# Tile columns of a two-layer encoder rounded up so that operands of full products start on 256-byte multiples

## The chip, the core and the metric

The kernel runs on one core of one Trainium2 chip. The metric is device time in microseconds (us) of one launch. Five engines work side by side: TensorE (PE in the profile; its weight loads stand under PEld), VectorE (DVE), ScalarE (ACT), GpSimd (POOL) and SyncE (SP, which only issues transfers here). TensorE reads both operands of a product from SBUF, the on-chip memory of 128 partitions, and writes to PSUM. A tile takes the same byte range in every partition, so its place is one number, its start within a partition. "Residue" below means this start modulo 256 bytes.

## The reference

Two layers of a transformer encoder over 256 tokens of width 1024, everything in float32. Each layer has a mixer and a channel part:

```
h    = rms_norm(x, n1); proj = h @ w_in                 # 1024 -> 2560
a: 4 heads, neighbourhood window with a bias table; q,k normed per head
d: 6 heads, three dilated windows joined by their log-sum-exp; partial rotary
c: 6 query heads on 2 key heads, full softmax; axial rotary
mix  = concat(rms_norm(out_a), rms_norm(out_d), rms_norm(out_c)) * gains
x    = x + mix @ w_out                                  # 1024 -> 1024
h    = rms_norm(x, n2); g, u = split(h @ w_gate_up)     # 1024 -> 2 x 2816
g    = depthwise_conv(g, 3 taps along the tokens) + conv_b
x    = x + (gelu(g) * u) @ w_down                       # 2816 -> 1024
```

## The kernel before, in words

Every large product is made in three terms. An operand z is split into z_hi, its value rounded to the type float32r, and z_lo = z - z_hi, also float32r; the product is hi·hi + hi·lo + lo·hi, added up in PSUM. The weights stream in from HBM in units of up to 2048 columns (tiles `wp_raw0` to `wp_raw3`); ACT rounds each unit into `wp_hi` and DVE subtracts into `wp_lo` (two buffers each, function `split`, lines 717 to 736). The profile names a product as output<-moving operand,stationary operand. These are the products of TensorE:

- Projections (lines 943 to 959): moving `wp_hi`/`wp_lo` with 384, 256 or 512 columns, stationary a 128x128 piece of `act_hT`, output in `psa_a`.
- Attention: transposes against `const_ident`, scores over 64 partitions (`act_ko`, `act_qo`, `act_kc`, `act_qc`), and weighted values (`act_pT` moving, `const_v` stationary), which are plain float32 and stand in the profile as two records each.
- Output projection (lines 967 to 984): moving `wp_hi`/`wp_lo` with 512 columns (in layer 2 partly `act_kc`/`act_qc`, reused as weight tiles), stationary `act_mixT_hi`/`act_mixT_lo`.
- Feed-forward up (lines 1370 to 1405, gate and up halves): a "large" term, moving `act_hT` with 512 columns (hi and lo side by side), stationary `wp_hi`, followed per output by a "little" term, moving 256 columns of `act_hT`, stationary `wp_lo`; eight of each per output half, in `psw_w`.
- Feed-forward down (lines 1457 to 1477): moving `wp_hi`/`wp_lo` with 512 columns, stationary `act_ch`/`act_cl`, the split activation; output in `psa_a`, one accumulation over all steps. The last piece is cut into 256 columns (line 1463).

The class `Plan` records all operations first, orders them with a cost model and a hand-tuned table of offsets (`PLACES`), and then emits them engine by engine (`order` and `emit`). It knows nothing of addresses. A tile's real place is taken at first use in `Slots.place` (lines 180 to 186), one allocation per buffer, sized in columns by the widest tile of that tag:

```
shape = list(t.shape) if self.dram else [P, BANK if self.psum else self.cols]
```

Allocations of SBUF follow one another, pool by pool (`const`, `wp`, `act`, `small`), each rounded up to 32 bytes. In the built program the first tile, `warm`, starts at byte 16512, and a few tiles whose size is no multiple of 256 bytes (`mh` 128 bytes, `gains` 192, `rot` 1664, `fo` one element, `few` 124, `sdq` and `sdk` 128, `cw` 352) shift everything behind them. Adding up the sizes gives these residues before:

| tiles | part in products | residue before |
|---|---|---|
| `const_ident`, `const_x` | moving and stationary of transposes | 0 |
| `wp_hi`, `wp_lo`, `wp_raw` | stationary (up), moving (projections, output, down) | 96 |
| `act_hT` | moving (up), stationary (projections) | 96 |
| `act_qo`, `act_ko`, `act_qc`, `act_kc`, `act_pT` | scores, values, some of the output projection | 224 |
| `act_mixT_hi`, `act_mixT_lo` | stationary (output projection) | 224 |
| `const_v6`, `const_v2` | stationary of the weighted values | 64 |
| `act_ch`, `act_cl` | stationary (down) | 64 |

Slices inside these tiles that a product reads step by multiples of 256 bytes, so all pieces of a tile share its residue.

Of the kernel before, what the change touches and what calls it, by code (L numbers as in the profile page):

```python
# [18 lines left out]
P = 128  # L19
# [17 lines left out]
UNIT = 2048  # L37
BANK = 512
NS2K = 5
NPT = 9  # L40

TURN_ACT = ("d", "dca")
# [128 lines left out]
class Slots:  # L171
# [7 lines left out]

    def place(self, t):  # L180
        if t.slot not in self.places:
            shape = list(t.shape) if self.dram else [P, BANK if self.psum else self.cols]
            self.places[t.slot] = self.pool.real.tile(
                shape, self.dtype, tag=f"{self.tag}{t.slot}", name=f"{self.pool.name}_{self.tag}{t.slot}", bufs=1
            )
        return self.places[t.slot]
# [86 lines left out]
class Plan:  # L273
# [5 lines left out]
    def pool(self, real, name, bufs, space=bass.MemoryType.SB):  # L279
        return PlanPool(self, real, name, bufs, space)  # L280
# [76 lines left out]
    def order(self):  # L357
# [82 lines left out]
        while len(done) < len(ops):  # L440
# [27 lines left out]
            for t in o.tiles:  # L468
                if t.slot is None:
                    s = t.pool  # L470
                    s.given += 1
                    place = min(s.free)
                    s.free.remove(place)
                    t.since, t.slot = taken_at(place[0], ""), place[1]
# [87 lines left out]
def encoder_kernel(  # L562
# [25 lines left out]
    const = pool("const", 1)  # L588
    wp = pool("wp", 3)
    act = pool("act", 2)  # L590
    small = pool("small", 4)
# [12 lines left out]

    gl0 = act.tile([16, P], F32, tag="s2k", name="gl0", bufs=NS2K)
    gl1 = act.tile([32, P], F32, tag="s2k", name="gl1", bufs=NS2K)
    gains = const.tile([P, 3, DEPTH, KD], F32, tag="gains", name="gains")
# [10 lines left out]
        nc.vector.tensor_copy(gains[:, i : i + n].rearrange("p a l k -> p (a l k)"), ps[:, :w])  # L618


    warm = const.tile([P, P], mybir.dt.bfloat16, tag="warm", name="warm")
    nc.gpsimd.memset(warm, 1.0)
    wps = psa.tile([P, WARM_W], F32, tag="a", name="wps")

# [163 lines left out]
    def mean_squares(name):  # L788

        ss = small.tile([P, NT, 2], F32, tag="ssx", name=f"ssx_{name}", bufs=2)  # L790
        for h in range(2):
            for t in range(NT):
                junk = act.tile([P, 512], F32, tag="s2k", name=f"sq_{name}{t}{h}", bufs=NS2K)
                nc.scalar.activation(
# [136 lines left out]
    for l in range(DEPTH):  # L931
# [84 lines left out]
        def normed(ps, nh, t, name):  # L1016

            w = nh * HD
            sq = act.tile([P, 512], F32, tag="s2k", name=f"sq_{name}", bufs=NS2K)
            ss = small.tile([P, 8], F32, tag="ss", name=f"ss_{name}")  # L1020
# [80 lines left out]
        class Head:  # L1101
# [4 lines left out]
            def softens(self, sps, whole):  # L1106

                name, bias = self.name, self.bias
                self.p = p = act.tile([P, NT, S], F32, tag="s2k", name=f"p_{name}", bufs=NS2K)
                nm = small.tile([P, NT], F32, tag="nm", name=f"nm_{name}")  # L1110
                rs = small.tile([P, NT], F32, tag="rs", name=f"rs_{name}")

                if bias is not None:
                    sb = act.tile([P, NT, S], F32, tag="s2k", name=f"sb_{name}", bufs=NS2K)
                    for t in range(NT):
# [22 lines left out]
            def turn(self):  # L1138
# [7 lines left out]
                odd = self.h % 2  # L1146
                self.pT = act.tile([P, NT, S], F32, tag="pT", name=f"pT_{name}", bufs=NPT)
                with nc.later(TURN_LATER):
# [436 lines left out]
```

## Time and profile before

| | us |
|---|---|
| median of 3 runs (lowest, highest) | 605.46 (604.07, 605.92) |
| the profiled execution, own time | 605.0 |
| its span, first to last instruction | 603.0 |
| PE busy in the span | 595.2 |
| PEld, DVE, ACT, POOL busy | 511.5, 471.1, 413.3, 78.0 |

The program runs on one core, and the granted TensorE clock is 1.000 over the whole span. A product's duration in the profile covers its pass through the array, and successive products overlap in it; the pace of a stream is read from the starts of its first and of the next product, divided by their count. The chain of waits merges neighbouring products to such pieces (start, length, count).

### The profile page before, as it was taken

The numbers are of one execution on the slowest core, as the hardware profiler recorded it, in microseconds if no ns is written. First come the engines' busy times: TensorE is split into PE (matmuls) and PEld (weight loads), VectorE is DVE, ScalarE is ACT, GpSimd is POOL, SyncE is SP. The second block draws the span as 40 slices with busy tenths as digits, with TensorE's granted clock in tenths as the row PEclk, the third lists the DMA queues.
The fourth block names the chain that finished last, engine by engine and source line by source line (L and its number), as shares of the span: only waits on it lengthen the run. The fifth ranks groups of instructions, "written<-read, shape, count | busy, mean of one in ns | idle before, by whom it ended". The sixth has DMA issues, their size and how long they took to land.

```text
span 603.0 us, 9676 instructions
## 1 busy us (share of the span) xinstructions
PE 595.2 (99%) x3423; PEld 511.5 (85%) x3423; DVE 471.1 (78%) x983; ACT 413.3 (69%) x1035; POOL 78.0 (13%) x124
## 2 busy tenths in 40 slices
PE   7999999999999999999999999999999999999997
PEld 6998787788888888888899988778888888888886
DVE  2788989897779797987977897668976677767875
ACT  4798989586575685756777898676765555646651
POOL 0652140160000000000014213421000000000000
PEclk9999999999999999999999999999999999999999
DMA  8896323555679898988635826944465455745511
GB/s 276 264 230 193 106 88 109 193 186 181 225 222 281 255 365 298 345 312 275 218 107 173 277 74 245 304 154 139 147 203 174 165 161 199 254 164 193 162 65 71
DMA packets 85216, 121.43 MB, mean 201 GB/s; under 512 B 9880, under 2 KB 69880, under 8 KB 85168
## 3 DMA queue, kind: packets, MB, share of 16 engines
q1 hardware_dynamic: 82992, 112.22, 57.2%
q0 software_dynamic: 1728, 8.39, 4.0%
q8 instruction: 27, 0.44, 0.3%
q10 hardware_dynamic: 448, 0.20, 0.1%
q14 instruction: 21, 0.17, 0.1%
HBM read 110.93 MB, written 9.88 MB: 200 GB/s over the span
## 4 chain that ended last, share of the span: by engine, by line
PE 92%; DMA 3%; DVE 2%; ACT 1%; issue 0%; POOL 0%; ACTq 0%; SPq 0%; DVEq 0%
PE psw_w L514 50%; PE psa_a L514 42%; DMA act_nab<-dram_scr 2%; DMA const_x<-in_x_dram 1%; DMA dram_scr<-act_nab 1%; DVE wp_lo L514 1%; ACT act_s2k L514 0%; DVE act_z L514 0%; DVE act_nab L514 0%; POOL small_rstd L514 0%; ACT wp_hi L514 0%; DVE act_sw L514 0%; ACT act_hT L514 0%; ACTq L514 0%; DVE act_s2k L514 0%
## 5 line engine op out<-in xcount | busy, mean ns | idle before, releaser
L514 DVE TENSOR_TENSOR wp_lo<-wp_raw,wp_hi 128x512 fp32r<-128x512 f32 (+2 forms) x332 | 233.8, 736 | 34.8 <-ACT wp_hi L514 19.3
L514 ACT CAST wp_hi<-wp_raw 128x512 fp32r<-128x512 f32 (+2 forms) x332 | 202.3, 666 | 19.0 <-PE psw_w L514 10.8
L514 PE MATMUL psw_w<-act_hT,wp_hi 128*128 128x512 f32 x704 | 182.8, 393 | 0.0
L514 PEld LDWEIGHTS psw_w<-act_hT,wp_hi 128*128 128x128 f32 x704 | 128.3, 188 | 23.9
L514 PE MATMUL psa_a<-wp_hi,act_hT 128*128 128x384 f32 (+2 forms) x448 | 114.6, 336 | 0.6 <-ACT wp_hi L514 0.6
L514 PEld LDWEIGHTS psw_w<-act_hT,wp_lo 128*128 128x128 f32 x704 | 100.2, 190 | 8.2
L514 PE MATMUL psw_w<-act_hT,wp_lo 128*128 128x256 f32 x704 | 105.2, 282 | 0.0
L514 PEld LDWEIGHTS psa_a<-wp_hi,act_hT 128*128 128x128 f32 x448 | 79.4, 191 | 3.8 <-ACT wp_hi L514 0.7
L514 PE MATMUL psa_a<-wp_lo,act_hT 128*128 128x384 f32 (+2 forms) x224 | 75.3, 338 | 0.0
L514 ACT COPY act_s2k<-psw_w 128x256 f32<-128x256 f32 x88 | 31.7, 372 | 57.5 <-PE psw_w L514 57.1
L514 DVE TENSOR_TENSOR act_s2k<-psw_w,act_s2k 128x256 f32<-128x256 f32 x88 | 36.1, 421 | 42.4 <-ACT act_s2k L514 41.9
L514 PE MATMUL psa_a<-wp_lo,act_ch 128*128 128x512 f32 (+1 forms) x176 | 68.6, 392 | 0.0
L514 PE MATMUL psa_a<-wp_hi,act_cl 128*128 128x512 f32 (+1 forms) x176 | 67.9, 392 | 0.0
L514 PE MATMUL psa_a<-wp_hi,act_ch 128*128 128x512 f32 (+1 forms) x176 | 65.9, 393 | 0.0
L514 PEld LDWEIGHTS psa_a<-wp_lo,act_hT 128*128 128x128 f32 x224 | 42.8, 191 | 2.3 <-DVE wp_lo L514 1.0
L514 PEld LDWEIGHTS psa_a<-wp_hi,act_cl 128*128 128x128 f32 x176 | 33.0, 188 | 7.0
L514 PEld LDWEIGHTS psa_a<-wp_lo,act_ch 128*128 128x128 f32 x176 | 32.9, 188 | 6.6
L514 PEld LDWEIGHTS psa_a<-wp_hi,act_ch 128*128 128x128 f32 x176 | 32.9, 188 | 6.6
L514 DVE SCALAR_TENSOR_TENSOR act_s2k<-act_s2k,act_cw,act_s2k 128x255 f32<-128x255 f32 x88 | 37.1, 478 | 0.0
L514 ACT ACTIVATE act_s2k<-act_s2k 128x512 f32<-128x512 f32 x22 | 13.9, 632 | 31.4 <-DVE act_s2k L514 31.4
L514 ACT ACTIVATE act_s2k<-act_s2k,act_cw 128x256 f32<-128x256 f32 x44 | 24.1, 596 | 14.9 <-DVE act_s2k L514 14.8
L514 POOL TENSOR_TENSOR small_rstd<-small_ms,const_mh 128x6 f32<-128x6 f32 (+2 forms) x26 | 31.3, 1204 | 15.8 <-DVE small_ms L514 14.1
(129 smaller groups left out, 710.7 us busy)
## 6 DMA issues: line engine op xcount, KB each, us to landing
wp_raw<-in_w_gate_up_dram SPq DMA_DIRECT2D x44, 1024.0 KB, 5.2
wp_raw<-in_w_down_dram SPq DMA_DIRECT2D x22, 1024.0 KB, 5.4
wp_raw<-in_w_in_dram SPq DMA_DIRECT2D x14, 768.0 KB, 4.6
wp_raw<-in_w_in_dram SPq DMA_DIRECT2D x8, 1024.0 KB, 5.4
wp_raw<-in_w_out_dram SPq DMA_DIRECT2D x8, 768.0 KB, 6.5
dram_khi<-act_mixT_hi SPq DMA_DIRECT2D x4, 768.0 KB, 5.0
dram_klo<-act_mixT_lo SPq DMA_DIRECT2D x4, 768.0 KB, 8.3
wp_lo<-dram_klo POOLq DMA_DIRECT2D x4, 768.0 KB, 5.7
```

The source lines that it names most:

```text
L514: getattr(o.engine.real, o.method)(*map(real, o.args), **{k: real(v) for k, v in o.kw.items()})
```

## The change

The number of columns of each allocation in SBUF is rounded up to a multiple of 64 elements (256 bytes in four-byte types), for all pools but `small`. The tile `warm`, in two-byte elements, is allocated with 192 columns (384 bytes) of which 128 are used, so that what follows its start at 16512 begins at 16896.

```diff
@@ constants of the module
 NS2K = 5
+EVEN = 64
 NPT = 9
@@ Slots.place
         if t.slot not in self.places:
-            shape = list(t.shape) if self.dram else [P, BANK if self.psum else self.cols]
+            cols = self.cols if self.pool.name == "small" else -(-self.cols // EVEN) * EVEN
+            shape = list(t.shape) if self.dram else [P, BANK if self.psum else cols]
@@ encoder_kernel
-    warm = const.tile([P, P], mybir.dt.bfloat16, tag="warm", name="warm")
+    warm = const.tile([P, 3 * EVEN], mybir.dt.bfloat16, tag="warm", name="warm")[:, :P]
```

No instruction is added or taken away, and the order of the instructions on every engine is the same row for row. Shapes, strides and sizes of transfers are the same. The starts move up by 256 bytes (`const_ident`, `const_x`) to 1216 bytes (`act_ch`), and every tile of the pools `const` (but `warm`), `wp` and `act` then has residue 0. Distances between tiles change only where a rounded tile lies between them: `wp` and `act_hT` keep theirs (61440 bytes from `wp_hi0` to `act_hT`), while `act_mixT_hi` lies 384 bytes and `act_ch` 544 bytes farther from `wp_hi0`.

## The prediction

> **What bounds the kernel now.** I read the first lines of the page first, then what TensorE waited for, then its pace stage by stage from the chain of waits and the timeline.
>
> ```profile
> span 603.0 us, 9676 instructions
> PE 595.2 (99%) x3423; PEld 511.5 (85%) x3423; DVE 471.1 (78%) x983; ACT 413.3 (69%) x1035; POOL 78.0 (13%) x124
> PEclk9999999999999999999999999999999999999999
> ...
> PE psw_w L514 <- DMA const_x<-in_x_dram: 1.9, 1, 1.9
> PE psa_a L514 <- POOL const_mh L514: 1.0, 1, 1.0
> PE psa_a L514 <- ACT wp_hi L514: 0.6, 1, 0.6
> ...
> 200.00:250.00 50.00, 50.00 (x265) 42.80 (x264) 43.54 (x76) 34.48 (x64) 0.00 (x0) 1.00 0.89 305
> ```
>
> TensorE is busy for 595.2 of 603.0 us, and its longest waits are 1.9, 1.0 and 0.6 us, at the start. The clock is whole. The last row is a stretch in the feed-forward of layer 1 with the columns PE, PEld, DVE, ACT, POOL, clock, DMA share and GB/s: no hole in PE, while DVE has 6.5 us to spare in 50. So the kernel's time is the sum of the paces of TensorE's products, and a change of layout counts only through them. These groups hold most of the products:
>
> ```profile
> L514 PE MATMUL psw_w<-act_hT,wp_hi 128*128 128x512 f32 x704 | 182.8, 393 | 0.0
> L514 PE MATMUL psw_w<-act_hT,wp_lo 128*128 128x256 f32 x704 | 105.2, 282 | 0.0
> L514 PE MATMUL psa_a<-wp_hi,act_hT 128*128 128x384 f32 x256 | 68.4, 344 | 0.6 <-ACT wp_hi L514 0.6
> L514 PE MATMUL psa_a<-wp_lo,act_ch 128*128 128x512 f32 x172 | 67.4, 395 | 0.0
> L514 PE MATMUL psa_a<-wp_lo,act_mixT_hi 128*128 128x512 f32 x56 | 22.4, 401 | 0.0
> ```
>
> The large up terms are 704, the down terms 3 x 172 = 516 (the other two of the three have the same count), the output projection 3 x 56 = 168 and 24 more with reused tiles.
>
> Do these paces depend on residues? The kernel before is its own experiment, since moving and stationary operands have equal residues in some stages and unequal ones in others. Timeline rows give start, length and tiles of a product or a row of them; the two pieces of the chain give start, length and count.
>
> ```profile
> 160.18 2.88 PE L514 MATMUL psw_w<-act_hT,wp_hi 128*128 128x512 f32 x12
> 162.90 0.28 PE L514 MATMUL psw_w<-act_hT,wp_lo 128*128 128x256 f32 x1
> ...
> 208.72 2.00 PE L514 MATMUL psw_w<-act_hT,wp_hi 128*128 128x512 f32 x8
> 210.56 0.52 PE L514 MATMUL psw_w<-act_hT,wp_lo 128*128 128x256 f32 x3
> ...
> 295.11 9.33 PE psa_a L514 x40
> 310.37 14.33 PE psa_a L514 x81
> ...
> 404.29 0.40 PE L514 MATMUL psa_a<-wp_hi,act_mixT_hi 128*128 128x512 f32 x1
> 404.53 0.39 PE L514 MATMUL psa_a<-wp_lo,act_mixT_hi 128*128 128x512 f32 x1
> 404.76 0.40 PE L514 MATMUL psa_a<-wp_hi,act_mixT_lo 128*128 128x512 f32 x1
> 404.99 0.39 PE L514 MATMUL psa_a<-wp_hi,act_mixT_hi 128*128 128x512 f32 x1
> ...
> 409.05 0.62 PE L514 MATMUL psa_a<-act_kc,act_mixT_hi 128*128 128x512 f32 x2
> 409.50 0.39 PE L514 MATMUL psa_a<-act_kc,act_mixT_lo 128*128 128x512 f32 x1
> 409.73 0.62 PE L514 MATMUL psa_a<-act_kc,act_mixT_hi 128*128 128x512 f32 x2
> 410.18 0.39 PE L514 MATMUL psa_a<-act_kc,act_mixT_lo 128*128 128x512 f32 x1
> 410.41 0.39 PE L514 MATMUL psa_a<-act_qc,act_mixT_hi 128*128 128x512 f32 x1
> ```
>
> All of these but the 81 stream 512 columns. Up, residues 96 and 96: 12 products from 160.18 to 162.90, **226.7 ns each**. Down, residues 96 and 64: 40 products in 9.33 us, **233.3 ns**. Output projection with `wp`, residues 96 and 224: from 404.29 to 404.99 three products, 233 ns. The same stage with `act_kc` as the moving tile, residues 224 and 224: six products from 409.05 to 410.41, 226.7 ns. The last pair is the telling one: same stage, same stationary tile, same shape, only another moving residue. Equal residues go at 226.7 ns, unequal ones at 233. The rows from 208.72 show the limit: eight up products with equal residues take 1.84 us, 230.0 ns each. They follow little terms, and such a run begins slower before it settles: 8 x 3.3 = 27 ns lost per run.
>
> **The change part by part.** Nothing is added, removed or reordered, and no transfer has another size. What changes is where operands begin: every residue becomes 0.
>
> (a) Down, 516 products: residues 96/64 become 0/0, that is, equal. If the pace of equal residues holds at 0, each gains 233.3 - 226.7 = 6.6 ns, 3.4 us in all. Below that stands the loss at the beginning of runs: at worst each run loses 27 ns at its beginning, and in the timeline the down products stand in 48 runs, 1.3 us. Bounds: 2.1 to 3.4 us gained; I take 2.5, since many runs follow large terms, which leave the pace settled.
>
> (b) Output projection, 168 products: 96/224 become 0/0. At best 168 x 6.6 = 1.1 us, at worst nothing, because transposes break these runs up and each restart is unsettled. I take 0.4.
>
> (c) Up, projections and scores, with equal residues now and then: only the common residue moves, from 96 or 224 to 0. The trace has no float32r product at residue 0. Nearest are the equal pairs 96/96 and 224/224, which have one pace, so I take nothing. The bounds are the rivals B and D below.
>
> (d) Last piece of down, cut to 256 columns, 24 products. Unequal residues, 597.92 to 599.21, go a little faster than equal ones in the little terms:
>
> ```profile
> 530.54 1.96 PE L514 MATMUL psw_w<-act_hT,wp_lo 128*128 128x256 f32 x15
> 532.33 0.40 PE L514 MATMUL psw_w<-act_hT,wp_hi 128*128 128x512 f32 x1
> ...
> 597.92 0.28 PE L514 MATMUL psw_w<-wp_hi,act_ch 128*128 128x256 f32 x1
> 598.04 0.28 PE L514 MATMUL psw_w<-wp_lo,act_ch 128*128 128x256 f32 x1
> 598.15 0.28 PE L514 MATMUL psw_w<-wp_hi,act_cl 128*128 128x256 f32 x1
> 598.27 0.28 PE L514 MATMUL psw_w<-wp_hi,act_ch 128*128 128x256 f32 x1
> 598.39 0.28 PE L514 MATMUL psw_w<-wp_lo,act_ch 128*128 128x256 f32 x1
> ```
>
> 1.79 us for 15 is 119.3 ns; 0.47 us for four is 117. Made equal they lose 24 x 2.5 = 0.06 us.
>
> (e) Transfers, ACT and DVE also meet new residues. Cost nothing: the weight loads run ahead of a TensorE that never waits for them after its first microseconds, and DVE has 6.5 us in 50 as cover. With that cover gone, each us that DVE falls behind would be one of TensorE; I see no row that asks for it.
>
> Sum: -2.5 - 0.4 + 0.06 = -2.8 us against the profiled execution's 605.0 (603.0 span and 2.0 around it), so 602.2. The median of the runs shown lies 0.5 above this execution, so the forecast for the median is **602.6 us**. By (a) and (b) at their ends it is 601.0 to 603.4.
>
> **The rivals.** A is the sum above: equality of residues is what counts.
>
> B: the start itself counts, and residue 0 streams faster. For it: 226.7 ns for 512 columns is not the floor of this TensorE. The weighted values stream a plain float32 tile, in twelve products of two 256-column records:
>
> ```profile
> 77.13 2.81 PE L514 MATMUL psw_w<-act_pT,const_v 128*64 128x256 f32 x24
> ...
> 399.72 1.04 PE L514 MATMUL psw_w<-const_ident,act_s2k 128*128 128x128 f32 x8
> 400.52 0.48 PE L514 MATMUL psa_a<-wp_lo,act_mixT_hi 128*128 128x512 f32 x1
> ```
>
> Less about 0.39 for the last one's own passage this is 2.42 us for eleven intervals, 220 ns per 512 columns. Against it: `act_pT` lies at residue 224, so a bad start did not cost this stream anything, and the eight transposes (100 ns each, and all bound by their 128-column loads) have stationary residues of 96 and 224 without a visible price. If float32r products reached 220: up 704 x (228 - 220) = 5.6, down 516 x 13.3 = 6.9, the other 288 with 512 columns x 11 = 3.2, the 384 projections with 384 columns, from the 81 in 14.33 us (177 ns) to 220 x 3/4 = 165, 4.6, and the 896 with 256 columns from 119 towards 110 (220/2) at most 8. That is 20 to 28 us, 577 to 585, about **580**.
>
> [...]
>
> C: no residue counts, and the time stays at **605.4**. The paces above would then follow from the kind of product before and after, not from addresses. For it: unsettled runs at 230 and more occur with equal residues too, as from 208.72, so down and output products might be slow because two of three products share a stationary piece or a moving one. Against it: `act_kc` against `wp` in one stage.
>
> [...]
>
> D, on the other side: the settled pace needs a common residue that is *not* 0. It is seen at 96 and 224 only, both an odd multiple of 32. The next product's weight load runs while this product streams (PEld is busy for 85% beside PE's 99%); if at residue 0 the two meet in the same part of the memory at every start, the up products and projections get the pace that down has now. Up would lose 704 x (233.3 - 228.5) = 3.4 us, where 228.5 is between settled and unsettled runs, the projections with 384 columns 384 x 6.6 = 2.5 at most, and down gains nothing: 605.5 + 3 to 6, **609**. It decides as soon as the settled up runs go above 230 ns.
>
> **How the numbers follow.** A 0.42, B 0.20, C 0.21, D 0.17. The likeliest gives 602.6, with its own range of 600.8 to 604. The range for 8 in 10 takes A, C and nearly all of D, and of B the mild half: 581 to 610. A measurement here tells differences over 0.3% (1.8 us) from none. Faster: B, and three quarters of A, since its lower end of 2.1 lies near that bound, 0.20 + 0.32 = 0.52. Same: the rest of A, most of C, 0.10 + 0.20 = 0.30. Slower: D and a remainder of C, 0.18.
>
> **What would show it.** Right: in the changed kernel's chain the long down pieces have 227 to 228 ns per product instead of 233.3, and the output projection has runs of 227 with `wp` as well; up keeps 226.7 settled and 230 behind little terms, and the projections keep 177. Wrong: up pieces of 12 products near 2.64 us (220 each) mean B; down pieces of 40 still at 9.3 us mean C; up pieces at 2.8 us mean D. PE waits over 1 us outside the start, or DVE at 50 of 50 in the feed-forward, would mean that the cover in (e) was too thin.

## The result and the profile after

| | us |
|---|---|
| before, median of 4 runs (lowest, highest) | 605.29 (604.07, 605.92) |
| after, median of 4 runs (lowest, highest) | 600.87 (600.74, 601.23) |
| after / before, 95% interval | 0.993 (0.9913 to 0.9948) |
| the profiled execution after: own time, span | 601.23, 599.4 |

The changed kernel is 4.4 us (0.7%) faster; the forecast was 602.6. The first lines of its page:

```profile
span 599.4 us, 9676 instructions
PE 590.7 (99%) x3423; PEld 510.8 (85%) x3423; DVE 471.2 (79%) x983; ACT 412.8 (69%) x1035; POOL 78.0 (13%) x124
PEclk8999999999999999999999999999999999999999
```

TensorE is still busy for 99% of the span: 4.5 us less in a span 3.6 us shorter, while the other engines do the same work in nearly the same time. Its chain of waits (start, length, piece, count) answers the pieces shown of before:

```profile
258.85 11.15 PE psw_w L516 x64
292.63 9.10 PE psa_a L516 x40
307.66 14.32 PE psa_a L516 x81
```

The down run of 40 went from 9.33 to 9.10 us, from 233.3 to 227.5 ns a product. The 81 projections stay at 177 ns, as before, and four rows of large and little up terms (each row eight large and eight little ones) take 11.15 us where before they took 11.18:

```profile
261.17 11.18 PE psw_w L514 x64
```

The timeline of TensorE after, at the other places of the prediction:

```profile
158.42 2.88 PE L516 MATMUL psw_w<-act_hT,wp_hi 128*128 128x512 f32 x12
161.14 0.76 PE L516 MATMUL psw_w<-act_hT,wp_lo 128*128 128x256 f32 x5
...
261.45 2.00 PE L516 MATMUL psw_w<-act_hT,wp_hi 128*128 128x512 f32 x8
263.29 1.12 PE L516 MATMUL psw_w<-act_hT,wp_lo 128*128 128x256 f32 x8
...
404.56 0.39 PE L516 MATMUL psa_a<-wp_lo,act_mixT_hi 128*128 128x512 f32 x1
...
405.69 0.39 PE L516 MATMUL psa_a<-act_kc,act_mixT_lo 128*128 128x512 f32 x1
...
593.57 0.28 PE L516 MATMUL psa_a<-wp_hi,act_ch 128*128 128x256 f32 x1
...
595.61 0.28 PE L516 MATMUL psw_w<-wp_hi,act_cl 128*128 128x256 f32 x1
```

Up: 12 in 2.72 us, 226.7 ns, and 8 behind little terms in 1.84 us, 230 ns: both unchanged. Output projection with `wp` moving: five intervals in 1.13 us, 226 ns instead of 233. Down's cut piece: 17 intervals in 2.04 us, 120 ns instead of 117.

Summed over all products from start to start, the changed kernel gains 2.27 us in down with 512 columns, 0.45 in the output projection and 0.21 in up's large terms, and loses 0.10 in the little ones and 0.05 in the cut piece: 2.8 us. That is the forecast gain. The rest of the 3.6, some 0.8 us, is a balance of waits: 0.5 us from the first 45 us, 0.6 from a wait near 54 us, where the interval of one projection product was 717 ns before and 120 after, and 0.4 lost to a longer wait near 382 us. The wait near 54 us before, in the rows of PE's waits (the changed kernel has no such row) and in the timeline:

```profile
PE psw_w L514 <- ACT act_s2k L514: 0.4, 1, 0.4
```

```profile
54.74 0.33 PE L514 MATMUL psw_w<-const_ident,act_s2k 128*128 128x128 f32 x1 [0.44 <-ACT act_s2k L514]
```

### The profile page after: what moved, and what is told of

Same layout as the page of the kernel before. It is cut to its first block, busy times and chain, and to the rows that moved or that the text cites. A ratio compares the mean times of both kernels' runs of the same rounds, so it can differ in the third digit from the quotient of the medians.

```text
span 599.4 us, 9676 instructions
## 1 busy us (share of the span) xinstructions
PE 590.7 (99%) x3423; PEld 510.8 (85%) x3423; DVE 471.2 (79%) x983; ACT 412.8 (69%) x1035; POOL 78.0 (13%) x124
## 4 chain that ended last, share of the span: by engine, by line
PE 94%; DMA 2%; ACT 1%; POOL 1%; issue 1%; DVE 0%; ACTq 0%; POOLq 0%
PE psw_w L516 50%; PE psa_a L516 45%; DMA wp_hi<-dram_khi 1%; DMA const_x<-in_x_dram 1%; ACT act_s2k L516 1%; POOL small_rstd L516 1%; POOL act_sqm L516 0%; ACT act_hT L516 0%; ACTq L516 0%; DVE small_ss L516 0%; DVE small_nm L516 0%; POOL wp_lo L516 0%; POOL small_ms L516 0%; DVE const_x L516 0%; ACT wp_hi L516 0%
## 5 line engine op out<-in xcount | busy, mean ns | idle before, releaser
L516 ACT CAST wp_hi<-wp_raw 128x512 fp32r<-128x512 f32 (+2 forms) x332 | 202.2, 666 | 18.3 <-PE psw_w L516 10.3
L516 ACT COPY act_s2k<-psw_w 128x256 f32<-128x256 f32 x88 | 31.6, 372 | 56.0 <-PE psw_w L516 55.6
L516 ACT ACTIVATE act_s2k<-act_s2k 128x512 f32<-128x512 f32 x22 | 13.9, 632 | 31.5 <-DVE act_s2k L516 31.4
L516 POOL TENSOR_TENSOR small_rstd<-small_ms,const_mh 128x6 f32<-128x6 f32 (+2 forms) x26 | 31.6, 1215 | 15.6 <-DVE small_ms L516 14.0
```

Of the source, the lines that this page charges most:

```text
L516: getattr(o.engine.real, o.method)(*map(real, o.args), **{k: real(v) for k, v in o.kw.items()})
```

## The experiments

The theory was that equal residues of the moving and the stationary operand set the pace. Its rivals were a faster residue 0 (B), no effect of residues (C), and a loss at a common 0 (D, which the unchanged 226.7 and 177 ns above had already struck out).

**A common residue other than 0.** The changed kernel with all tiles behind `fo` 96 bytes further, so that all full float32r products keep equal residues, at 96:

```
             cols = self.cols if self.pool.name == "small" else -(-self.cols // EVEN) * EVEN
+            cols += 24 if self.tag == "fo" else 0
```

> The changed kernel with one tile 96 bytes larger ahead of the weight tiles: all tiles of the pools wp and act then share residue 96 instead of 0; only the transposes' identity, x and the stationary values keep 0. Theory 'difference' (what counts is that moving and stationary operand have equal residues): nothing changes against the changed kernel, 600.9 us within 1, and the chain's down piece of 40 products stays at 9.10 us (227.5 ns each). Theory 'start' (an operand that begins on a multiple of 256 bytes streams faster): the time goes back to that of before, 605.3, and the piece of 40 to 9.33 us. If the 256-byte starts help the transfers, the time lies between with the piece at 9.10.

It took 602.19 us, 0.995 of before (0.9932 to 0.9968). Its chain of waits:

```profile
293.36 9.10 PE psa_a L517 x40
308.38 14.32 PE psa_a L517 x81
```

These are the changed kernel's 227.5 and 177 ns. Residue 0 is not faster than 96: B falls. The total was 1.3 us above the changed kernel's, and since the paces were the same, both were timed once more side by side.

> The changed kernel itself once more, on one chip with the next two. Its paces account for 2.8 us of its gain; the first timing gave 4.4. If the rest was an accident of that timing, it is now 602.3 within 0.5 beside 605.2; if a common residue of 0 has something that 96 lacks (shorter transfers), it is 1 us or more below the kernel with common residue 96.

> All weight and activation tiles at residue 96 once more, for the comparison with the changed kernel in the same call. 'Only the difference counts': the two agree within 0.5 us. 'Transfers gain from 256-byte starts': this one is 1 us or more slower, with the same TensorE paces.

600.54 us (ratio 0.9939, 0.9919 to 0.9958) and 601.39 us (0.9945, 0.9929 to 0.9961), again with equal paces. The kernel before took 604.67 us beside them, so the changed kernel's gain is 4.1 us here: more than its paces account for, as in the first timing. Between the two, the intervals overlap; these runs alone don't tell whether the 0.85 us are real. The last two experiments return to it.

**Down alone, both ways.** The changed kernel with `act_ch` and `act_cl` at 224, which makes down unequal again:

```
             cols = self.cols if self.pool.name == "small" else -(-self.cols // EVEN) * EVEN
+            cols += 56 if self.tag == "rb" else 0
```

and the kernel before with them at 96, which makes down alone equal:

```
-            shape = list(t.shape) if self.dram else [P, BANK if self.psum else self.cols]
+            cols = self.cols + (8 if self.tag == "rb" else 0)
+            shape = list(t.shape) if self.dram else [P, BANK if self.psum else cols]
```

> The changed kernel with the tile ahead of act_ch 224 bytes larger: act_ch and act_cl at residue 224, all else at 0, so that down has the difference of before (moving 32 bytes above stationary, modulo 256) and nothing else is undone. 'Difference': down back to 233 ns, its 516 products cost 516 x 4.4 (228.65 to 233.05 ns in the two traces) = 2.3 us more, 603.2 us; up, projections and output projection as in the changed kernel. 'Start of the moving operand': down stays at 227.5 ns and the time at 600.9.

> The kernel before with one tile, rb, 32 bytes larger: act_ch and act_cl move from residue 64 to 96, the residue of the weight tiles; every other tile that a product reads stays where it was. 'Difference': down goes to 227.5 ns, the time falls by 2.3 us to 603.0. 'Start': no operand gets to a multiple of 256, the time stays at 605.3 and down at 233 ns.

Times: 603.44 us (0.9974, 0.9961 to 0.9988) and 603.25 us (0.9973, 0.9956 to 0.9989). The chain of waits of the first:

```profile
292.58 9.33 PE psa_a L517 x40
```

and of the second:

```profile
296.74 9.10 PE psa_a L515 x40
```

In these four layouts the pace of down follows the equality of its two residues: 233.3 ns at 0/224, as at 96/64, and 227.5 at 96/96, as at 0/0. C falls. Of the 4.4 us, down made equal alone gives 2.0 (against 605.22 for the kernel before beside it), and down made unequal costs 2.6 in the changed kernel, a difference between two separate timings (2.1 to 3.3 by the ratios of the changed kernel's three timings). The 2.3 that the starts of its products show lies between.

**The pace pair by pair.** A kernel without the encoder: TensorE alone, rows of 24 products for each pair of residues.

> A kernel that only measures: no encoder is computed, the output is filled with sums that mean nothing. TensorE alone runs float32r products in runs of 24, moving tiles at residues 0, 4, 16, 32, 64 and 128, stationary tiles at sixteen residues from 0 to 240, first with 512 columns and then (moving 0, 32, 64) with 256; then eight products of 256 columns at each stationary residue followed by ten equal ones of 512 columns; then 24 bf16 products. 'Difference': with 512 columns the settled pace is 226.7 ns where the residues are equal and 230 to 235 ns where they differ by 32 or 128, whatever the moving one is. 'Start': the pace depends on the moving residue alone, and 0 is the fastest. [...] bf16: 216 ns, so that the 226.7 would be float32r's own.

TensorE's timeline in it (`mv` and `st` are the moving and the stationary tile with their residues; a row's pace is the next row's start less its own, over 24):

```profile
26.10 5.61 PE L612 MATMUL even<-mv0b,st0b 128*128 128x512 f32 x24
31.55 5.74 PE L612 MATMUL odd<-mv0b,st4b 128*128 128x512 f32 x24
...
48.26 5.75 PE L612 MATMUL even<-mv0b,st32b 128*128 128x512 f32 x24
53.85 5.76 PE L612 MATMUL odd<-mv0b,st48b 128*128 128x512 f32 x24
...
120.85 5.90 PE L612 MATMUL odd<-mv4b,st4b 128*128 128x512 f32 x24
126.59 5.85 PE L612 MATMUL even<-mv4b,st8b 128*128 128x512 f32 x24
...
417.26 5.60 PE L612 MATMUL even<-mv64b,st64b 128*128 128x512 f32 x24
422.70 5.61 PE L612 MATMUL odd<-mv64b,st80b 128*128 128x512 f32 x24
...
749.62 5.13 PE L625 MATMUL bf<-half 128*128 128x512 bf16 x23
```

0/0: 227 ns; 0/32: 233; 4/4: 239; 64/64: 227. Over the last 12 of each row, all equal pairs at 0, 32, 64 and 128 go at 226.7 and most unequal ones at 233, with exceptions: a moving tile 64 bytes above the stationary one 228.6 to 228.9, and some pairs 16 bytes apart 226.7. The two moving residues tried that are no multiple of 32 behave differently: at 16 the equal pair has 231.2, and some unequal ones 226.7; at 4 every partner gives 235 to 240. So at these two the start does count by itself. Bfloat16 goes at 216. So 226.7 is the best settled pace of float32r among these pairs; none comes near 220.

**What is left in up.** Eight large terms behind little ones begin unsettled even with equal residues: 230 ns above, against 226.7 for twelve. In the map, rows of 256 columns go at 113.3 ns with the stationary tile 64 bytes above the moving one and at 120 when equal, so `wp_lo` was put at 64 in the whole changed kernel:

```
+            cols += {"hi": 16, "lo": 48}.get(self.tag, 0)
```

> The changed kernel with wp_lo at residue 64 and all else at 0. From the map: little terms (moving 0, stationary 64) go at 113.3 ns in a long run instead of 119.5, but at 118 when eight of them follow products of 512 columns, and products of 512 columns with moving 64 and stationary 0 at 228.9 instead of 226.7. If the long-run pace is reached, the 704 little terms gain 704 x 5.5 = 3.9 us, the third of down with wp_lo loses 172 x 2.2 = 0.4 us: 3.5 us below the changed kernel. If the state left by the large terms decides, the gain is 0 to 1 us and down's loss is kept: no difference, or slower by 1 us.

No gain: 602.51 us (0.996, 0.9944 to 0.9975), 2.0 us above the changed kernel's 600.54 beside it in the medians and 1.3 by the ratios, with intervals that overlap. The second branch of the expectation came out, somewhat worse than stated. Its chain of waits:

```profile
258.51 11.12 PE psw_w L517 x64
292.28 9.28 PE psa_a L517 x40
```

Little terms gained (83.65 to 82.44 us in all), but down, which streams `wp_lo` as every third moving operand, went to 232 ns and lost 1.8, and up's large terms 0.4. The paces seen in rows of one pair, 113.3 ns for little terms and 228.9 for a moving `wp_lo`, did not carry over to these mixes. So the next kernel, again without the encoder, ran the program's own mixes (up, down, projections) on TensorE alone for sixteen places of `wp_lo`.

> Again a kernel that only measures and computes no encoder. TensorE alone runs the program's own patterns and addresses: six times eight large up terms and eight little ones, then 24 down products in the order hi, lo, hi, then 24 projection products of 384 columns in the same order, all for wp_lo at sixteen residues in steps of 16, everything else at 0. If the unsettled runs of the program come from other engines, they are missing here: up terms 226.7 throughout. If TensorE makes them itself, a piece of eight large terms behind little ones takes 1.84 us here as well (230 each), at wp_lo residue 0. For down at residue 0: 24 x 226.7 = 5.44 us; at 64: 5.5; at the others 5.5 to 5.6.

Its timeline of TensorE, for `wp_lo` at 0 and at 208:

```profile
27.21 2.00 PE L608 MATMUL upb<-hT,hib 128*128 128x512 f32 x8
29.05 1.12 PE L608 MATMUL upb<-hT,lo0b 128*128 128x256 f32 x8
30.00 0.40 PE L608 MATMUL upa<-hT,hib 128*128 128x512 f32 x1
...
366.08 1.99 PE L608 MATMUL upb<-hT,hib 128*128 128x512 f32 x8
367.91 1.09 PE L608 MATMUL upb<-hT,lo208b 128*128 128x256 f32 x8
368.84 1.99 PE L608 MATMUL upa<-hT,hib 128*128 128x512 f32 x8
```

At 0 a row of eight and eight takes 2.79 us, large terms 1.84 as in the program, though this kernel gives the other engines only loads and copies ahead of the products and stores behind them: the unsettled beginnings need none of the encoder's other work. At 208 it takes 2.76, the least of the sixteen once the rows repeat; 24 down products take 5.47 us at 0 and 5.56 at 208. Up and down want different places, and one tile can give each its own: the last version puts only up's pieces of `wp_lo` at 208.

```
-        lo = wp.tile([P, UNIT], F32R, tag="lo", name=f"lo{i}", bufs=PARTS)
+        lo = wp.tile([P, UNIT + 64], F32R, tag="lo", name=f"lo{i}", bufs=PARTS)
+        off = 52 if i % PER_LAYER >= LAST_OUT and b == 2 * P else 0
+        lo = lo[:, off : off + UNIT]
```

> The changed kernel with one edit: the low pieces of the up units alone begin 208 bytes behind a multiple of 256 (their tiles are 64 elements longer, and only these units use columns 52 to 2099); every other operand, the low pieces of down included, stays at residue 0. It keeps apart what v1_lo64 mixed: down keeps equal residues, and only the stationary piece of up's little terms moves. Theory, that TensorE's own pace depends on the residues of the moving and the stationary operand and on the ones just before: in the record of m2_orders a row of eight large and eight little terms took 2793.5 ns with this piece at residue 0 and 2760 at 208, so 88 such rows gain 88 x 33.5 = 2.9 us: some 597.6 us beside the changed kernel at 600.5, large terms near 1826 instead of 1841 ns per row of eight, little ones near 117, down runs unchanged at 227.5. Rival, that the other engines' accesses, absent in m2_orders, set part of these paces: up stays within 0.5 us of the changed kernel's. Rival on the other side: what stands between (split writes at an odd start, other orders of large and little terms) loses as in v1_lo64: 601 to 603.

> The changed kernel as it is, beside v2_up_lo208 on one chip: 600.5 us by every theory, with 600.2 to 601.3 as in its executions so far.

It took **599.17 us** (0.9885 of before, 0.9864 to 0.9906), and the changed kernel beside it 601.14 (0.992, 0.9897 to 0.9943): 2.0 us better in the medians, faster than both kernels, with intervals that just overlap. Its six executions lie from 598.48 to 599.95, those of the changed kernel from 600.22 to 602.05. Its chain of waits:

```profile
259.20 11.03 PE psw_w L516 x64
292.69 9.08 PE psa_a L516 x40
```

Four rows of up and little terms went from 11.15 to 11.03 us, down is kept. Against the changed kernel beside it, the starts of the products give 2.05 us in up and little terms and 0.35 in down, which was expected unchanged; why down gained is not shown. The 2.9 expected counted all 88 rows as whole, while in the program only 28 rows of eight and eight stand unbroken.

**The table that transfers write.** The pace sum of 2.8 us leaves 1.6 of the 4.4 unexplained, and the wait near 54 us was a lead: followed back, it hangs on DVE's work on `act_nab`, the bias table, for which DVE waited before:

```profile
48.46 1.43 DVE L514 SCALAR_TENSOR_TENSOR act_nab<-act_nab,const_na 128x576 f32<-128x576 f32 x2 [1.71 <-DMA act_nab<-dram_scr]
```

and not after:

```profile
46.18 1.42 DVE L516 SCALAR_TENSOR_TENSOR act_nab<-act_nab,const_na 128x576 f32<-128x576 f32 x2
```

Two strided transfers write it in 3,584 packets of 256 bytes. At 224, as before, every packet crosses a multiple of 256 bytes (the expectation below says every second, which is wrong: 256 bytes that start anywhere but at 0 cross one); at 0 none does. No product reads this tile, so it can be moved alone: to 224 in the changed kernel, to 0 in the kernel before.

```
-        nabs[l] = act.tile([P, RPB_C, GRID_W], F32, tag="nab", name=f"nab{l}", bufs=1)
+        nab = act.tile([P, RPB_C * GRID_W + 64], F32, tag="nab", name=f"nab{l}", bufs=1)
+        nabs[l] = nab[:, 56 : 56 + RPB_C * GRID_W].rearrange("p (r c) -> p r c", c=GRID_W)
```

(8 in place of 56 in the kernel before.)

> The changed kernel with one tile moved back: act_nab, the table that a transfer writes in 3,584 packets of 256 bytes between 38 and 47 us, begins at residue 224 as before (its tile is 64 elements longer, and columns 56 and up are used); TensorE does not read it, and all its operands stay at residue 0. Theory: at residue 224 every second of these packets crosses a multiple of 256 bytes. In the records of the kernels with this tile at 96 or 224 they took 28.7 to 31.6 ns each, DVE began with the table 10.5 us or more after the first of these transfers was issued, and the first layer's products then waited 0.4 to 2.7 us for act_s2k from ACT; with the tile at 0 19.6 to 24.3 ns, 9.1 to 10.0 us, and no such wait, but for 0.6 in v2_up_lo208. So: packets near 29 ns, a wait of 0.4 to 1 us for act_s2k, paces as in the changed kernel, some 601 to 601.8 us. Rival: something else decides when the table lands (the place of the weight tiles, how late the start was): packets stay near 20 ns, no wait, 600.5 to 601.2.

> The kernel before with one tile moved: act_nab begins at residue 0 (8 elements further, the tile 64 longer); all else, the operands of TensorE included, stays where it was. Theory, as for e4_after_nab224: packets of 256 bytes near 20 to 24 ns instead of 30 to 32, DVE begins with the table 9 to 10 us after its issue, the wait for act_s2k is gone, paces unchanged, the down runs at 233.3: 0.4 to 1 us under the kernel before. Rival: packets stay near 30 ns, the wait stays, and the time is that of the kernel before. By either theory this alone is within what a measurement here can tell from no change, so the packets and the wait in its record decide.

The row of the DMA queue in a stretch of 1.5 us within these packets (packets, MB, the time they took as a share of 16 engines; 42.5 to 44 us, in the last kernel, whose packets pause there, 43.5 to 45), before:

```profile
q1 hardware_dynamic: 996, 0.25, 135.6%
```

after:

```profile
q1 hardware_dynamic: 1279, 0.32, 102.1%
```

changed kernel with the table at 224:

```profile
q1 hardware_dynamic: 991, 0.25, 134.9%
```

kernel before with the table at 0:

```profile
q1 hardware_dynamic: 1533, 0.39, 118.9%
```

Share times 24 us over packets gives 32.7, 19.2, 32.7 and 18.6 ns a packet in these stretches. Stretches differ, so the mean over all 3,584 packets is the better measure: 31.6 ns before and 19.6 after, 31.5 in the changed kernel with the table at 224 and 20.4 in the kernel before with it at 0. In all twelve records of the encoder it is 28.7 to 31.6 with the table at 96 or 224 and 19.6 to 24.3 with it at 0: the mean length follows the residue of this one tile, both ways. The first 200 of these packets take 18 ns each both before and after; the difference shows later: those that start from 42 to 43 us take 36.3 ns before and 18.3 after. By which path the place of the written tile lengthens them is not shown.

Times: the changed kernel with the table at 224 took 602.34 us (0.9957, 0.9937 to 0.9978), where without that edit its ratios were 0.993, 0.9939 and 0.992; the kernel before with the table at 0 took 603.53 us, 0.9966 of before (0.9948 to 0.9984). So the tile is worth 2.0 us in the kernel before (1.0 to 3.1 by the interval), and by the ratios some 1.1 to 2.2 us in the changed one, where the intervals overlap. Part of the 2.0 may be the granted clock: among executions with 0.999 or more the medians are 605.1 (13 of the kernel before) and 603.8 (6 with the table at 0), 1.3 us apart. That is about what was unexplained, and it may also account for the 0.85 us between the common residues 96 and 0, where the table crossed too; that is argued, not shown.

Where are these microseconds lost within one execution? The DVE rows on the table, and the transfers' issue ahead of them, in the timeline of the changed kernel with the table at 224:

```profile
37.26 2.30 SPq L516 DMA_DIRECT2D act_nab<-dram_scr  x2
47.46 1.48 DVE L516 SCALAR_TENSOR_TENSOR act_nab<-act_nab,const_na 128x576 f32<-128x576 f32 x2 [0.99 <-DMA act_nab<-dram_scr]
```

and in that of the kernel before with the table at 0:

```profile
36.96 5.59 SPq L514 DMA_DIRECT2D act_nab<-dram_scr  x2
47.25 1.43 DVE L514 SCALAR_TENSOR_TENSOR act_nab<-act_nab,const_na 128x576 f32<-128x576 f32 x2 [1.34 <-DMA act_nab<-dram_scr]
```

10.2 and 10.3 us from issue to use, nearly alike, though the packets are not; in the second kernel the two issues lie 3.3 us further apart. So these two records miss what was expected of them: the first has no wait for `act_s2k`, and the second has one interval of 388 ns where the others have 120. The wait changes from record to record: in the kernel before with down made equal it was the longest of all,

```profile
PE psw_w L515 <- ACT act_s2k L515: 2.7, 1, 2.7
```

All twelve records together show the place. TensorE runs the same products in the same order in all of them, so each record can be laid beside the changed kernel's, product by product. The table gives when DVE begins with the table (on the changed kernel's time: less what TensorE already lies behind or ahead at 50 us) and what TensorE loses between the products near 54 and 55 us:

| kernel | table at | DVE begins, us | lost near 54 us |
|---|---|---|---|
| before | 224 | 47.9 | 0.65 |
| before, down made equal | 224 | 50.2 | 3.1 |
| changed, table moved | 224 | 47.2 | 0.0 |
| changed, common residue 96, two records | 96 | 48.0, 48.5 | 0.7, 1.2 |
| before, table moved | 0 | 47.6 | 0.3 |
| changed, three records | 0 | 46.2, 46.2, 47.3 | 0.0, 0.0, 0.0 |
| changed, down made unequal | 0 | 47.3 | 0.0 |
| changed, `wp_lo` at 64 | 0 | 46.2 | 0.0 |
| changed, up's `wp_lo` at 208 | 0 | 47.1 | 0.8 |

In these records the lateness of the table costs nothing up to 47.3 us; beyond it, TensorE loses about what DVE is late (0.3 us at 47.6, 3.1 at 50.2). The last row is another wait: there DVE stood 0.87 us for POOL's `small_rstd`. Of five records with the table off a multiple of 256 four lose time here through the table, of seven with it at 0 one, by 0.3 us. So the loss lies near 54 us and hangs on when the table lands, and DVE tends to begin later with a misaligned table (47.2 to 50.2 us, at 0 46.2 to 47.6); the changed kernel with the table at 224, with 47.2 and no loss, shows that it need not. One record of each kernel can't give its mean: the size of the term rests on the timed medians.

## Why the prediction came out, and what it missed

The forecast 602.6 was 1.7 us high. The part that was forecast, the paces of TensorE's products, came out at 2.8 us as summed; what is missing is a term put at nothing. By its steps:

- **(a) Down, 2.5 us: held.** Measured 2.27 by starts, 2.0 and 2.6 by doing it alone and undoing it. The reading that carried it, two moving residues in one stage at 233 and 226.7 ns, was confirmed by every equal pair tried at a multiple of 32, all at 226.7; the equal pair at 16, with 231.2, is outside it.
- **(b) Output projection, 0.4: held,** 0.45.
- **(c) Up, projections and scores, nothing: held** within 0.2 us; settled 226.7, unsettled 230 and the projections' 177 ns came out as named. The unsettled runs, taken there as a fact of restarts, are a matter of residues as well: with `wp_lo` at 208 behind them they shrink, eight large terms from 1.84 us (the changed kernel's timeline from 261.45) to 1.82 (from 261.79 in the version with up's `wp_lo` at 208).
- **(d) The cut piece, a loss of 0.06: held,** 0.05.
- **(e) Transfers at nothing: the step that failed.** "The weight loads run ahead" was right for the weights, whose packets of 1024 bytes had about the same length at both residues (50.3 ns before, 49.6 after). It overlooked a transfer in small packets that does not run ahead: the table, written late by a trip through DRAM (4.83 us out and 9.65 us back in the chain of before), with DVE, then ACT, then TensorE behind it. Its own row of waits (ACT `act_s2k`, 0.4) was in the view, below the three rows that the prediction quoted. Nor was DVE's spare time a cover here: DVE itself stood 1.71 us waiting for the table. Made aligned, the table was worth 1 to 2 us by the medians.

Of the rivals, B fell by the common residue 96 and by the row 0/0 at 226.7 ns; in the map only bfloat16 went faster, at 216. That the eight transposes named against B hang on their weight loads shows in the record before: PEld is busy for all 0.80 us from 399.72 to 400.52, where in the up row from 160.18 it is for 2.25 of 2.72. C fell by the kernel before with only down made equal. D fell by the changed kernel's own settled rows. The range, 581 to 610, was much wider than needed on the fast side: the stream of weighted values, plain float32, was no evidence that float32r can go at 220.

## What to carry to other kernels

Where TensorE is the bound, read the pace of each kind of product from the starts of its rows, and compare it with the residues modulo 256 bytes of both operands: equal residues at 0, 32, 64 or 128 gave long rows of 512 columns in float32r their best pace here (226.7 ns, most unequal pairs 233), but rows that alternate between shapes had places of their own (eight and eight: 2.79 us with `wp_lo` at 0, 2.76 at 208), found on the mix and not on one pair. An operand's place can be chosen per use by a column offset inside a slightly longer tile. Where a layout changes, look also at transfers in packets of 256 bytes (here 31.6 ns each into a tile at 224, 19.6 into one at 0) and at what waits for them, not only at the engine that bounds the kernel.

## What was not expected of the hardware

- The stationary operand's place alone changes the pace of the products: 226.7 ns at 0/0 and 233 at 0/32, as at 64/64 and 64/32, with the same moving tile and shape and no encoder beside them; by which path is not shown.
- The paces repeat: eight large terms behind little ones take 1.84 us in the records before and after, and a row of eight and eight takes 2.79 us in the program (11.15 us for four) as in the kernel that holds only these mixes.
- For rows of 256 columns an equal pair is among the slow ones: 120 ns at 0/0, 32/32 and 64/64, as at 0/128, and 113.3 to 113.4 with the stationary tile 64 bytes above the moving one.
- With the moving tile at residue 4 a product takes 235 to 240 ns, up to 6% over the settled 226.7.
- The table's packets of 256 bytes take 19.6 to 24.3 ns in the mean of a record where they start on a multiple of 256 bytes, and 28.7 to 31.6 where they start 96 or 224 behind one, though the first of them take 18 ns both before (224) and after (0).
